# Attention outputs kept feature by token: no turns back, softmax sums and row scales applied as broadcast rows and columns

## The chip, the cores and the metric

One Trainium2 chip, and of it one core. The metric is the device time of one execution in microseconds. The kernel before takes 1211.41 us (median of three runs, 1211.18 to 1212.05).

## The reference

One transformer block over 1024 tokens and 1024 features. Half of the mixed width is attention (8 heads of 64), half is a gated recurrence (HGRN, 4 heads of 128).

```python
h = rmsnorm(x, mix_pre_norm[layer])
proj = h @ w_in[layer]
...
attn = dilated_mixture_attention(q_a.reshape(ahead), k_a.reshape(ahead), v_a.reshape(ahead), slopes)
attn = rmsnorm(attn.reshape(B, S, ATTN_WIDTH), attn_out_norm[layer])
rec = hgrn2_recurrence(q_h, f_h, i_h, g_h, lower_bounds[layer], hgrn_out_norm[layer])
mixed = jnp.concatenate([attn, rec], axis=-1) @ w_out[layer]
x = x + rmsnorm(mixed, mix_post_norm[layer])
h = rmsnorm(x, mlp_pre_norm[layer])
ff = jnp.square(jax.nn.relu(h @ w_ff1[layer])) @ w_ff2[layer]
x = x + rmsnorm(ff, mlp_post_norm[layer])
```

The attention mixes three patterns (dilations 1, 4 and 16), each a softmax over blocks, by their softmax sums. So for each token and head there is one sum of exponentials by which the output is divided, and for each token one row scale `ra` of the norm over all 512 attention features, with a gain for each feature.

## The kernel before

All large products are float32 in three passes: both operands are split into a rounded half (hi) and the rest (lo), and `three_pass` (L88 to L91) multiplies hi by hi, lo by hi and hi by lo. ACT rounds (L85) and DVE or POOL subtracts (L86).

The work has these stages: the projections and the recurrence; the eight attention heads in 64 steps (about 310 to 515 us); the output product, its norm and the residual by eight tiles of 128 tokens (515 to 591 us); and the two MLP products. PE runs one queue of instructions whose order the code writes by hand. A step s = 8 * head + i handles one of eight items (D0 to D3 for the first 512 tokens; F0, F1, N0, N1 for the others) of a head: scores for the coming item (`raise_`), their masked maximum on DVE (`look`), the exponential on ACT (L894), turns of the probabilities on PE (`turn`, L904 to L916), the products with the values (`weigh`), and in a later step `finish`. Between them `fill` puts pieces of a queue of other products into PE's order (keys and values of coming heads, and in the last heads `early_out`: the recurrent half of the output product of tiles 0 to 3, tiles `pwe`). The table `hooks` adds loads and passes at given steps. Steps 56 to 63 are head 7.

`weigh` gives the output of two heads' values as features by tokens, in PSUM. The value rows are split as well, so 128 partitions hold the hi part's and the lo part's product (64 each). ACT copies them into SBUF. `finish` (L978 to L996) turns 128 tokens at a time back by `TE.transpose` (L988: 2, 2 and 4 per head, 64 in all), DVE adds the two parts (L992), and POOL multiplies by the reciprocal `rd` of the softmax sums, which then are one number per token and so one per partition (L993). Pairs of heads collect in `anat` slabs and go to `mix_dram`, tokens by 1024 features; the last pair stays in SBUF.

The sums of the F items lie in another order of tokens than the rest. `send` (step 5) writes them to DRAM with their order changed, `receive` (step 6) reads them back (`swd`, `stat`, L856 and L859), and `finish` of the last item, in step 1 of the next head, adds them (L985) and takes the reciprocal. Two more tiles, `swap` (L867) and `px` (L875), carry row maxima to PE and back.

The output stage takes the attention features of a tile from `mix_dram` (`row_load`), sums their squares on ACT (`row_norm`), takes the scale on POOL, multiplies by the gain (POOL) and, for tiles 4 to 7, by the scale (`row_attn`, DVE), and turns the 512 features back by four transposes (`row_turn(t, 1)`, L1080, 32 in all), splitting them into hi and lo. `late_out` multiplies: 12 matmuls per half tile for tiles 0 to 3, whose recurrent half is there already, and 24 for tiles 4 to 7. `mixed_half` adds (tiles 0 to 3, with the scale) and squares for the norm behind it. `residual` and `next_turn` (tiles `ph`, `hraw`, `h2`) prepare the MLP for the tiles that are done.

DMAs go out from SP in one queue, in the order in which the code writes them, each behind the waits of the one ahead. Each of them uses one of eight semaphores in turn, so it also waits for the landing of the eighth before it. ACT, DVE and POOL work off one queue each, in order too.

## Time and profile before

| | |
|---|---|
| median of three runs | 1211.41 us |
| the profiled execution, its span | 1210.78 us, 1209.0 us |
| PE busy | 1198.8 us (99%) |
| DVE, ACT, POOL busy | 868.8, 546.6, 328.9 us |
| granted TensorE clock | 1.00 |
| heads, output loop | to 515.08 us; 515.08 to 591.21 us |

The span runs from the first to the last instruction. In lists of groups "x32" is a count and three numbers of a duration are shortest, median and longest, in ns. In timelines the first column is the start, the second the time busy, and brackets hold the idle time ahead and who ended it. Where a row carries several matmuls, its time runs from the first start to the last end. In the list of DMAs the last number is the time from issue to landing.

### The profile page before, as it was taken

Reading aid. Unit: us, or ns where it says so; the run is one execution under the profiler, and the core shown is the slowest. Engines: PE = TensorE matmul, PEld = TensorE weight load, DVE = VectorE, ACT = ScalarE, POOL = GpSimd, SP = SyncE. Lnnn points to the kernel's source line nnn. Section 1 sums busy time; section 2 is a strip of 40 time slices with the busy share of each in tenths; the row PEclk is TensorE's granted clock in tenths of the full one; section 3 lists DMA queues with packets and bytes.
Section 4 is the critical chain, followed back from the end, with each engine's and each line's share of the span. In section 5 each row is a group of like instructions: output and inputs, shape, how many; then the busy total and the mean of one; then the engine's idle time right before and its main releaser. Section 6 shows DMA issues by size and latency. Waiting matters only on the chain.

```text
span 1209.0 us, 17248 instructions
## 1 busy us (share of the span) xinstructions
PE 1198.8 (99%) x6350; PEld 1027.1 (85%) x6350; DVE 868.8 (72%) x1476; ACT 546.6 (45%) x1067; POOL 328.9 (27%) x323
## 2 busy tenths in 40 slices
PE   9999999999999999999999999999999999999998
PEld 8898989888888887888888888888888888888886
DVE  5697978777666767677689566766688554578796
ACT  7633333322665668855664222222234543534562
POOL 0110201022221215264330786575631000000022
PEclk9999999999999999999999999999999999999999
DMA  6231323123434445263514555553587534433337
GB/s 219 69 95 57 107 73 109 36 82 87 139 93 124 126 126 142 94 228 125 191 62 157 183 196 192 202 182 143 205 318 267 200 102 142 163 98 104 106 105 279
DMA packets 85716, 173.17 MB, mean 143 GB/s; under 512 B 12416, under 2 KB 38016, under 8 KB 85632
## 3 DMA queue, kind: packets, MB, share of 16 engines
q1 hardware_dynamic: 85632, 172.07, 42.9%
q8 instruction: 50, 0.82, 0.3%
q14 instruction: 34, 0.28, 0.1%
HBM read 117.76 MB, written 47.99 MB: 137 GB/s over the span
## 4 chain that ended last, share of the span: by engine, by line
PE 95%; ACT 2%; DVE 2%; issue 1%; POOL 0%; DVEq 0%; POOLq 0%; ACTq 0%
PE f L1947 18%; PE f2s L1947 7%; PE pig L91 2%; PE pig L89 2%; PE pig L90 2%; PE pl L480 2%; PE pwo L89 2%; PE pwo L91 2%; PE pwo L90 2%; PE pm_ak L89 1%; PE pm_f L89 1%; PE pm_ak L91 1%; PE pm_ak L90 1%; PE pm_f L91 1%; PE pm_f L90 1%; PE pm_av L89 1%
## 5 line engine op out<-in xcount | busy, mean ns | idle before, releaser
L86 DVE TENSOR_TENSOR al<-ar,ah 128x1024 fp32r<-128x1024 f32 x56 | 70.6, 1260 | 79.2 <-ACT ah L85 79.2
L1947 PE MATMUL f<-bh,ah 128*128 128x512 f32 x320 | 124.5, 389 | 0.0
L1947 PE MATMUL f<-bl,ah 128*128 128x512 f32 x320 | 124.5, 389 | 0.0
L1947 PE MATMUL f<-bh,al 128*128 128x512 f32 x320 | 124.5, 389 | 0.0
L85 ACT ACTIVATE ah<-ar 128x1024 fp32r<-128x1024 f32 x56 | 59.1, 1056 | 83.9 <-DMA ar<-actd 78.5
L1947 PEld LDWEIGHTS f<-bh,ah 128*128 128x128 f32 x320 | 60.1, 188 | 12.6
L1947 PEld LDWEIGHTS f<-bl,ah 128*128 128x128 f32 x320 | 60.1, 188 | 12.5
L1947 PEld LDWEIGHTS f<-bh,al 128*128 128x128 f32 x320 | 60.1, 188 | 12.3
L2021 POOL TENSOR_SCALAR lbl<-ssq 128x1 f32<-128x1 f32 x4 | 3.3, 820 | 245.7 <-ACT fd L2017 245.6
L1570 POOL TENSOR_TENSOR e<-x,e 128x512 f32<-128x512 f32 x14 | 21.6, 1540 | 131.0 <-DVE x L1521 131.0
L1947 PE MATMUL f2s<-bh,al 128*128 128x512 f32 (+1 forms) x128 | 48.9, 382 | 0.0
L1947 PE MATMUL f2s<-bl,ah 128*128 128x512 f32 (+1 forms) x128 | 48.9, 382 | 0.0
L1947 PE MATMUL f2s<-bh,ah 128*128 128x512 f32 (+1 forms) x128 | 48.9, 382 | 0.0
L673 POOL COPY tout<-traw 128x256 f32<-128x256 f32 x16 | 12.7, 792 | 106.6 <-DMA traw<-in_bias_tab_dram 76.2
L86 DVE TENSOR_TENSOR bl<-br,bh 128x1024 fp32r<-128x1024 f32 x32 | 40.1, 1252 | 1.4 <-ACT bh L85 1.3
L1964 ACT ACTIVATE acc<-f 128x512 f32<-128x512 f32 x28 | 16.7, 598 | 50.1 <-PE f L1947 50.1
L993 POOL TENSOR_TENSOR anat<-anat,stat 128x128 f32<-128x128 f32 (+1 forms) x24 | 12.4, 515 | 92.4 <-DVE anat L992 78.7
L85 ACT ACTIVATE bh<-br 128x1024 fp32r<-128x1024 f32 x32 | 33.6, 1051 | 5.0 <-PE f L1947 3.3
L86 DVE TENSOR_TENSOR wl<-raw,wh 128x1024 fp32r<-128x1024 f32 x21 | 27.2, 1295 | 8.9 <-ACT wh L85 8.9
L709 POOL TENSOR_TENSOR kl<-kf,kh 64x512 fp32r<-64x512 f32 x16 | 22.2, 1389 | 39.6 <-ACT kh L708 37.4
L753 POOL TENSOR_TENSOR ql<-qf,q 64x512 fp32r<-64x512 f32 x16 | 21.4, 1339 | 41.6 <-ACT q L752 41.0
L89 PE MATMUL pwo<-woh,mt 128*128 128x512 f32 x80 | 32.2, 402 | 0.0
(1703 smaller groups left out, 4030.0 us busy)
## 6 DMA issues: line engine op xcount, KB each, us to landing
ar<-actd SPq DMA_DIRECT2D x56, 512.0 KB, 3.5
br<-in_w_ff_dram SPq DMA_DIRECT2D x16, 1024.0 KB, 6.1
w1r<-in_w_ff_dram SPq DMA_DIRECT2D x14, 1024.0 KB, 6.4
raw<-in_w_in_dram SPq DMA_DIRECT2D x26, 512.0 KB, 3.6
actd<-e SPq DMA_DIRECT2D x17, 768.0 KB, 4.3
actd<-e SPq DMA_DIRECT2D x11, 1024.0 KB, 4.1
raw<-in_w_out_dram SPq DMA_DIRECT2D x8, 512.0 KB, 3.6
xres<-in_x_dram SPq DMA_DIRECT2D x8, 512.0 KB, 4.2
```

The costliest lines, as they stand in the source:

```text
L85: S.activation(hi, src, AF.Copy)
L86: eng.tensor_tensor(out=lo, in0=src, in1=f32(hi), op=ALU.subtract)
L89: TE.matmul(dst, lhs[0], rhs[0], start=start, stop=False)
L90: TE.matmul(dst, lhs[0], rhs[1], start=False, stop=False)
L91: TE.matmul(dst, lhs[1], rhs[0], start=False, stop=stop)
L480: TE.matmul(pl[:, n % 2, :192], kt[:, n * P:(n + 1) * P], sets[u // 2][:, n % 4], start=True, stop=True)
L673: G.tensor_copy(by_class(dst[:, part_ * w:(part_ + 1) * w]), in_blocks(raw[:, FAR * DIL:]))
L709: G.tensor_tensor(out=kl[a:b], in0=src, in1=f32(kh[a:b]), op=ALU.subtract)
L753: G.tensor_tensor(out=lo[a:b], in0=full[a:b], in1=f32(stacks[i]["q"][a:b, sl]), op=ALU.subtract)
L1570: eng[0].tensor_tensor(out=e1[:, 3], in0=a21, in1=e1[:, 2], op=ALU.add)
L1947: TE.matmul(pm, a[:, j, c], b[:, j, d], start=start and j == 0 and q == 0, stop=stop and j == 1 and q == 2, skip_group_check=True)
L1964: S.activation(acc_at(p, i), pm, AF.Copy)
```

## The change

`weigh` and `finish` no longer turn. ACT copies the 64 partitions of one part, and `finish` is one add on DVE, into a slab `o` of features by tokens for each pair of heads. The reciprocals go to DRAM as rows (`rd_dram`, 512 elements of 4 bytes a time) by `send_rows`, at step 3 for the first 512 tokens and at step 7 for the others, each from SP; the add that needs the received sums now stands there, at the end of step 7. The slabs of pairs 0 to 2 go to `o_dram`. `out_load` reads a pair back (`on`, 512 KB) with its reciprocals broadcast over 64 partitions per head (`rdr`, two of 256 KB). `out_scale` multiplies the two (POOL, 128x1024), `out_square` sums squares of the pairs into `osq` (POOL), `out_split` applies the gain as a column and splits (ACT and DVE), and its results go into the products as they are. `out_norm` gets the row scales by four 128x1 matmuls of `osq` with ones. Tiles 0 to 3 are scaled behind the product, as before. For tiles 4 to 7 the recurrent half is divided by the scale in PSUM (`late_rec`, ACT, both halves of a tile first), the attention half added on top, and the common factor goes into the `eps` of the norm behind.

```diff
     def weigh(hd, kind, g):
...
-            S.activation(ot, po[:, :256], AF.Copy)
+            S.activation(ot[a:b], po[c:d, :256], AF.Copy)
...
     def finish(hd, kind, g, po, ot):
...
-        if kind == "N":
-            V.tensor_tensor(out=st["xd"], in0=st["dn"][:, 4:8], in1=st["xd"], op=ALU.add)
-            V.reciprocal(st["rd"][:, 4:], st["xd"])
-        for u in range(n):
-            TE.transpose(po[:, o + u * P:o + (u + 1) * P], ot[:, u * P:(u + 1) * P], ident)
...
-        V.tensor_reduce(dst, pair.rearrange("p u a d -> p u d a"), axis=AX.X, op=ALU.add)
-        G.tensor_tensor(out=dst, in0=dst, in1=st["rd"][:, b].unsqueeze(2).to_broadcast([P, n, 64]), op=ALU.mult)
+        if kind == "D":
+            dst, src = outs[pr][a:b, g * 256:g * 256 + 256], po[a:b, :256]
+            V.tensor_tensor(out=dst, in0=src, in1=ot[a:b], op=ALU.add)
...
+        if hd % 2 and kind == "N" and pr < AH // 2 - 1:
+            nc.sync.dma_start(out=o_dram[pr], in_=outs[pr])
+
+    def send_rows(hd, hf):
+        st = stats[hd]
+        sl = slice(4 * hf, 4 * hf + 4)
+        if hf == 1:
             V.tensor_tensor(out=st["xd"], in0=st["dn"][:, 4:8], in1=st["xd"], op=ALU.add)
+            V.reciprocal(st["rd"][:, sl], st["xd"])
+        nc.sync.dma_start(out=rd_dram[hd][sl].rearrange("b p -> p b"), in_=st["rd"][:, sl])
...
+    def out_load(pr, hfs=(0, 1)):
+        if pr < AH // 2 - 1:
+            outs[pr] = slab("S", f"on{pr}")
+            nc.sync.dma_start(out=outs[pr], in_=o_dram[pr])
+        if 0 in hfs:
+            loaded[pr] = slab("S", f"rdr{pr}")
+        c = slice(512 * hfs[0], 512 * hfs[-1] + 512)
+        for i, (a, b) in enumerate(halves):
+            nc.sync.dma_start(out=loaded[pr][a:b, c], in_=rd_dram[2 * pr + i].rearrange("b p -> (b p)")[c].partition_broadcast(64))
+
+    def out_scale(pr, c=slice(0, T), eng=G):
+        eng.tensor_tensor(out=outs[pr][:, c], in0=outs[pr][:, c], in1=loaded[pr][:, c], op=ALU.mult)
+
+    def out_square(pr, c=slice(0, T), eng=G):
+        o = outs[pr][:, c]
+        if pr == 0:
+            scales["osq"] = slab("S", "osq")
+            eng.tensor_tensor(out=scales["osq"], in0=o, in1=o, op=ALU.mult)
             return
+        sq = loaded[pr][:, c]
+        eng.tensor_tensor(out=sq, in0=o, in1=o, op=ALU.mult)
+        eng.tensor_tensor(out=scales["osq"][:, c], in0=scales["osq"][:, c], in1=sq, op=ALU.add)
+
+    def out_split(pr, hf):
+        hi, lo = out_part(pr, hf)
+        src, gain = outs[pr][:, hf * 512:hf * 512 + 512], gains["cols"][:, pr:pr + 1]
+        S.activation(hi, src, AF.Copy, scale=gain)
+        V.scalar_tensor_tensor(lo, src, gain, f32(hi), op0=ALU.mult, op1=ALU.subtract)
+
+    def out_norm(hf):
+        pn = bank("t", f"pn{hf}")
+        for j in range(4):
+            t = 4 * hf + j
+            TE.matmul(pn[:, j:j + 1], scales["osq"][:, t * P:(t + 1) * P], f32(ones), start=True, stop=True)
...
+    def late_rec(t, hf):
...
+        for j in range(4):
+            three_pass(pm, [mts[t][:, i, j] for i in range(2)], [w[:, sl] for w in parts[WO0 + j]], j == 0, j == 3)
+        S.activation(pm, pm, AF.Copy, scale=scales["row", 1][:, t - NE:t - NE + 1])
...
-        55: lambda: [w_get(WO0 + 4, 0), row_load(0)],
-        57: lambda: [row_load(1), row_norm(0, (0,))],
...
+        51: lambda: out_load(0),
+        52: lambda: [row_turn(2), load_gain("gmix", "R", g_mix)],
+        53: lambda: [out_scale(0), out_square(0)],
+        54: lambda: [row_turn(3), out_split(0, 0), out_split(0, 1)],
+        55: lambda: out_load(1),
+        56: lambda: [out_scale(1), out_square(1)],
+        57: lambda: [out_split(1, 0), out_split(1, 1), out_load(2)],
+        58: lambda: out_scale(2),
+        59: lambda: [w_get(WO0 + 4, 0), out_square(2), out_split(2, 0)],
+        61: lambda: [w_get(WO0 + 5, 0), out_load(3, (0,))],
+        63: lambda: [w_get(WO0 + 6, 0), out_scale(3, FIRST), out_square(3, FIRST), out_split(3, 0)],
...
+        elif i == 7:
+            send_rows(hd, 1)
...
+    out_load(3, (1,))
     w_get(WO0 + 7, 0)
-    row_norm(2)
-    row_gain(2)
+    out_norm(0)
+    out_split(2, 1)
...
     for t in range(NT):
-        late_out(t, 0, last_rows if t == 0 else None)
+        if t >= NE:
+            late_rec(t, 0)
+            late_rec(t, 1)
+        late_out(t, 0)
+        if t == 0:
+            out_scale(3, SECOND, V)
+            out_square(3, SECOND)
+            out_split(3, 1)
+        elif t == 1:
+            out_norm(1)
```

The queue of SP around head 6's sums, first before (`etable` is a table of biases, `gmix` the gains as rows, `swd6` and `stat6` head 6's sums out and in, `raw` weights):

```order
L800 DMA etable_4793<-tabd7_643 128x704
L1004 DMA gmix_5290<-in_g_mix_dram 128x1024
L856 DMA swd6_650<-stat6_5012 128x4
L859 DMA stat6_5012<-swd6_650 128x4x1
L106 DMA raw34_5389<-in_w_out_dram 128x1024
L1030 DMA row0_5391<-mixd_135 128x384
```

and now (`rdd6` is head 6's reciprocals, sent in two parts; `on` and `rdr` as above):

```order
L803 DMA etable_4767<-tabd7_644 128x704
L1267 DMA cols_88<-in_g_mix_dram 128x4x1
L1003 DMA rdd6_662<-stat6_4974 128x4x1
L1058 DMA on0_5213<-od0_653 128x1024
L1063 DMA rdr0_5215<-rdd0_656 64x1024
L1063 DMA rdr0_5215<-rdd1_657 64x1024
L1011 DMA gmix_5254<-in_g_mix_dram 128x1024
L859 DMA swd6_651<-stat6_4974 128x4
L862 DMA stat6_4974<-swd6_651 128x4x1
L1003 DMA rdd6_662<-stat6_4974 128x4x1
L1058 DMA on1_5357<-od1_654 128x1024
L1063 DMA rdr1_5359<-rdd2_658 64x1024
```

Five DMAs have come in between `etable` and `gmix`, and the loads of pair 1 stand behind the second `rdd6`, which needs `stat6`.

The queue of ACT at step 57, in head 7, before (`pd7` to `pf7` are exponentials, `pth7` the rounded halves of turned probabilities, `dm0` a sum of squares over a loaded row):

```order
L933 ACTIVATE pth7_0_5412<-pt7_D1_5449 128x2x128
L1046 ACTIVATE dm0_5476,ass_5475<-row0_5391 128x384
L894 ACTIVATE pd7_5327,stat7_5326<-pd7_5327,stat7_5326 128x512
L933 ACTIVATE pth7_2_5496<-pt7_D2_5495 128x3x128
L953 ACTIVATE pf7_5328<-pov7_0_5506 128x256
L1046 ACTIVATE dm1_5513,ass_5512<-row1_5473 128x384
L894 ACTIVATE pf7_5328,stat7_5326<-pf7_5328,stat7_5326 128x192
L933 ACTIVATE pth7_2_5496<-pt7_D3_5521 128x4x128
```

and now:

```order
L936 ACTIVATE pth7_0_5381<-pt7_D1_5421 128x2x128
L1081 ACTIVATE othh_5043<-on1_5357,cols_88 128x512
L1081 ACTIVATE ot0_5327<-on1_5357,cols_88 128x512
L897 ACTIVATE pd7_5291,stat7_5290<-pd7_5291,stat7_5290 128x512
L936 ACTIVATE pth7_2_5465<-pt7_D2_5464 128x3x128
L958 ACTIVATE pf7_5292<-pov7_0_5475 64x256
L897 ACTIVATE pf7_5292,stat7_5290<-pf7_5292,stat7_5290 128x192
L936 ACTIVATE pth7_2_5465<-pt7_D3_5488 128x4x128
```

In the place of one pass over `row0` stand two over the scaled pair 1, ahead of the exponential `pd7` and the two `pth7` that PE's items use.

The queue of ACT in tile 6 of the output loop, before (`dx50` squares the residual of tile 5, `hraw` copies turned tiles out of PSUM, `dp60` squares the mixed tile 6, `h2h` rounds):

```order
L1161 ACTIVATE dx50_6350,x2h_6349<-xres5_6213 128x512
L1161 ACTIVATE dx51_6355,x2h_6349<-xres5_6213 128x512
L1192 ACTIVATE hraw00_6012<-ph23_0_6364 128x4x128
L1192 ACTIVATE hraw10_6021<-ph23_1_6370 128x4x128
L1132 ACTIVATE dp60_6377,pss_6376<-pwo6_0_6305 128x512
L1192 ACTIVATE hraw01_6409<-ph24_0_6404 128x4x128
L1192 ACTIVATE hraw11_6416<-ph24_1_6411 128x4x128
L1132 ACTIVATE dp61_6420,pss_6376<-pwo6_1_6379 128x512
L85 ACTIVATE h2h0_6013<-hraw00_6012 128x4x256
L85 ACTIVATE h2h1_6022<-hraw10_6021 128x4x256
```

and now:

```order
L1183 ACTIVATE dx50_6210,x2h_6209<-xres5_6087 128x512
L1183 ACTIVATE dx51_6215,x2h_6209<-xres5_6087 128x512
L1214 ACTIVATE hraw00_5900<-ph23_0_6224 128x4x128
L1214 ACTIVATE hraw10_5909<-ph23_1_6230 128x4x128
L1154 ACTIVATE dp60_6237,pss_6236<-pwo6_0_6157 128x512
L1214 ACTIVATE hraw01_6256<-ph24_0_6251 128x4x128
L1214 ACTIVATE hraw11_6263<-ph24_1_6258 128x4x128
L1154 ACTIVATE dp61_6267,pss_6236<-pwo6_1_6171 128x512
L1129 ACTIVATE pwo7_0_6275<-pwo7_0_6275,ora1_5748 128x512
L1129 ACTIVATE pwo7_1_6289<-pwo7_1_6289,ora1_5748 128x512
L86 ACTIVATE h2h0_5901<-hraw00_5900 128x4x256
L86 ACTIVATE h2h1_5910<-hraw10_5909 128x4x256
```

The two scalings of the recurrent halves of tile 7 (L1129) have come ahead of `h2h0`.

In PE's queue the four matmuls of `out_norm(0)` (L1088) now stand between the last `weigh` and the first product of tile 0, which followed it at once before.

189 lines of the change are left out of this document (78 added, 111 removed).

## The prediction

> **What bounds the kernel now.** I read the first part of the page (PE 99% busy, in the table above), then the busy time by stretch, then the list of PE's waits, then the timelines.
>
> ```profile
> 475.00:515.00 40.00, 39.26 (x256) 33.94 (x254) 27.41 (x85) 32.05 (x91) 11.33 (x19) 1.00 0.40 120
> 515.00:591.00 76.00, 76.00 (x385) 63.79 (x384) 56.01 (x73) 42.06 (x112) 35.68 (x69) 1.00 0.48 165
> ```
>
> The columns of the two stretches are the length and then the busy time of PE, PEld, DVE, ACT and POOL. PE is never idle in the output loop (515 to 591) and idle for 0.74 us in the last 40 us of the heads, where ACT is busy for 32 of 40. So a PE instruction taken away is time gained, and a PE wait put in is time lost. Between 300 and 606 us PE's waits are these and one of 0.2:
>
> ```profile
> PE pwe L89 <- DVE vf L766: 0.7, 1, 0.7
> PE pt_F L916 <- ACT pf L894: 0.6, 1, 0.6
> PE px L875 <- DVE swap L867: 0.3, 1, 0.3
> ```
>
> That is 1.8 us in total. There is almost no waiting to remove, and the margins behind it are thin: ACT and DVE deliver a few tenths of a microsecond ahead of PE.
>
> **What goes on PE.** Both kinds of turn are seen between three-pass matmuls.
>
> ```profile
> L988 PE MATMUL pov_far<-ident,pn x32: 271/273/273, 337.0 to 516.8; 128*128 128x128 f32 x32
> L988 PE MATMUL pov<-ident,pf x16: 270/272/273, 316.4 to 502.6; 128*128 128x128 f32 x16
> L988 PE MATMUL pov<-ident,pd x16: 272/283/299, 323.0 to 508.7; 128*128 128x128 f32 x16
> L1080 PE MATMUL pmt<-ident,row x48: 270/273/297, 511.2 to 572.2; 128*128 128x128 f32 x48
> ...
> 502.53 0.38 PE L988 MATMUL pov<-ident,pf 128*128 128x128 f32 x2
> 502.67 0.48 PE L89 MATMUL pwe<-wh,emt 128*128 128x512 f32 x1
> ...
> 516.51 0.60 PE L988 MATMUL pov_far<-ident,pn 128*128 128x128 f32 x4
> 516.94 0.60 PE L1080 MATMUL pmt<-ident,row 128*128 128x128 f32 x4
> 517.30 0.47 PE L89 MATMUL pwo<-woh,mt 128*128 128x512 f32 x1
> 517.61 0.39 PE L90 MATMUL pwo<-wol,mt 128*128 128x512 f32 x1
> 517.84 0.39 PE L91 MATMUL pwo<-woh,mt 128*128 128x512 f32 x1
> ```
>
> The durations (0.27 us) overlap; the starts give the price. Matmuls follow each other by 0.23 (517.61 to 517.84), but the one behind turns holds 0.31 (517.30 to 517.61). Two turns take 0.14 (502.53 to 502.67); with the 0.08, 0.22 a pair. Eight take 0.79 and the same 0.08: 0.87, so 0.44 for four. The 64 turns of `finish` go: 16 pairs, 3.5 us, and 8 fours, 3.5. The attention half of every output row is not turned: 32 of the 48 turns of L1080, 8 fours, 3.5 us. The eight 128x1 matmuls of `out_norm` come.
>
> ```profile
> 501.23 0.28 PE L875 MATMUL px<-pick,swap 128*128 128x4 f32 x2
> 501.37 0.63 PE L904 MATMUL pt_D<-ident,pd 128*128 128x128 f32 x4
> ```
>
> The nearest is this pair of 128x4, 0.14 us; so 0.6 us for eight, between nothing and the 0.9 of eight turns. Net 10.5 - 0.6 = **9.9 us less PE work**, of which 3.2 us lie in the output loop (8 fours less the second `out_norm`). The three-pass products keep their number and shape. POOL's small products (L993) and DVE's reductions (L992) go too, on engines with time to spare.
>
> **First new wait: DVE in heads 1 to 5.** `send_rows(hd, 1)` puts the add that needs the joined sums `xd` at the end of step 7; until now it stood two steps later.
>
> ```profile
> 366.40 0.16 DVE L985 TENSOR_TENSOR stat<-stat 128x4 f32<-128x4 f32 x1
> ...
> 357.95 0.38 SPq L859 DMA_DIRECT2D stat<-swd  x1
> ...
> 360.30 0.42 DVE L844 CUSTOM_DVE_ANT_0 pn<-ps_N,bt 128x256 f32<-128x256 f32 x1 [1.10 <-PE ps_N L840]
> ...
> DMA to landing us min/median/max: 1.4/3.4/5.8
> ```
>
> For head 1 the receive leaves at 357.95 and lands 3.4 later, at 361.4; the add is now ahead of the score pass of 360.30, which waits 1.1 us, and PE's next scores wait for its bank. Bounds: nothing, to 2.5 us a head. I take 2.8 for five heads. It hardly counts, because of what follows.
>
> **Second: the chain of head 6.** In the last head ACT's `out_split`, in its one queue, waits for POOL's `out_scale`, and that for two loads, which stand behind `send_rows(6, 1)` on SP.
>
> ```profile
> 480.03 0.43 SPq L995 DMA_DIRECT2D mixd<-anat  x1
> 480.51 0.58 SPq L800 DMA_DIRECT2D etable<-tabd  x1
> 482.78 0.56 SPq L856 DMA_DIRECT2D swd<-stat  x1
> ...
> gmix<-in_g_mix_dram SPq DMA_DIRECT2D x1, 512.0 KB, 7.3
> ...
> swd<-stat SPq DMA_DIRECT2D x1, 2.0 KB, 5.8
> stat<-swd SPq DMA_DIRECT2D x1, 2.0 KB, 2.3
> ...
> DMA to landing us min/median/max: 5.0/5.8/6.6
> L86 POOL TENSOR_TENSOR wl<-raw,wh 128x1024 fp32r<-128x1024 f32 x2 | 4.8, 2394 | 5.3 <-ACT wh L85 5.3
> ```
>
> Five more DMAs (`cols`, a send, `on0`, two `rdr0`) stand ahead of `swd6`, each 0.48 behind the last (480.03 to 480.51): it leaves at 485.2 and not 482.78. It lands 5.8 later, 491.0; the receive 2.3 later, 493.3; add and reciprocal 0.4; then the send, `on1` and two `rdr1`, the last issued at 495.1. A 256 KB broadcast (the smaller of the two `etable` rows) lands in 5.0: 500.1. Bounds are 2.3 (a small row that meets an idle queue) and `gmix`' 7.3. POOL multiplies 128x1024 in 2.4: 502.5. ACT splits a half in 0.6, DVE follows with 0.7 for each of two halves: 504.4 (estimates from the 128x512 passes of both engines). DVE then has score passes and the sums of head 7 to do before the `swap` of PE's second `px`:
>
> ```profile
> 499.24 0.36 DVE L844 CUSTOM_DVE_ANT_0 pf<-ps_F,etable 128x192 f32<-128x192 f32 x1 [0.26 <-PE ps_F L840]
> ...
> 500.19 0.38 DVE L867 TENSOR_TENSOR swap<-stat,pick 128x128 f32<-128x128 f32 x1
> ```
>
> That is 1.3 us: PE's `px` starts at 505.7, where it now starts at 501.23. Without the chain it would have come 6.5 us early less the first waits, near 498.5. **So all that PE saved until here is lost, and 4.5 us more**, whatever its exact amount. The first `out_scale` (step 54) waits in the same way, 2 us, and lies inside this.
>
> **Third: the norm ahead of the products.**
>
> ```profile
> 515.08 0.45 PE L89 MATMUL pwo<-woh,mt 128*128 128x512 f32 x1
> ...
> 511.63 0.33 SPq L106 DMA_DIRECT2D raw<-in_w_out_dram  x1
> ...
> L1037 POOL TENSOR_TENSOR erows<-erows,etable x4: 1285/1340/2311, 457.0 to 477.9; 128x512 f32<-128x512 f32 x4
> ```
>
> From `px` to the first product are 13.85 us now, 0.9 less without two pairs and a four; POOL is still busy with pair 1 (two squares of 2.4) when ACT asks for pair 2, 0.9 us more. The heads would end at 519.5. But `out_norm(0)` needs pair 3's first half scaled, squared and added by POOL, and its `rdr3` is loaded behind `raw35` on SP, 511.63 + 4.5 + 0.9 = 517.0, so issued by 517.8. I let it land in the 3.4 of the middle `swd` row, 521.2, and POOL takes three times 1.34: 525.2. PE waits 5.7 us. With the four small matmuls the products start at 525.5, **10.4 us later than now**. Bounds: 2 us of waiting, if the row lands at once and POOL keeps to 1.28; 9 if it lands in 5 and POOL takes 1.9.
>
> **The output loop.** It has 3.2 us less PE work, but `late_rec` puts both recurrent halves of tiles 4 to 7 first, and their PSUM scaling (L1129) into ACT's queue.
>
> ```profile
> 572.30 1.04 PE L1186 MATMUL ph<-ident,esum 128*128 128x128 f32 x8
> ...
> 578.64 1.04 PE L1186 MATMUL ph<-ident,xres 128*128 128x128 f32 x8
> ...
> 577.60 1.06 ACT L1192 ACTIVATE hraw<-ph 128x512 f32<-128x512 f32 x2
> ...
> 580.82 2.02 ACT L85 ACTIVATE h2h<-hraw 128x1024 fp32r<-128x1024 f32 x2
> ...
> 590.41 1.22 DVE L86 TENSOR_TENSOR wl<-raw,wh 128x1024 fp32r<-128x1024 f32 x1
> ```
>
> Between the turns of tile 3 (572.30) and of tile 4 (578.64), which share banks, stand 24 matmuls; now 12, 2.8 us less. ACT's first copy out of the bank ends at 578.13, 0.5 ahead of PE, and it waits for DVE's residual and not for PE: PE waits 2.2. Then `h2h`, 2.2 us behind 578.64, comes to stand behind the scaling of `pwo7_1`, that is 24 matmuls, some 7.2 us behind; the `wl` that it delays by 5.0 ends at 591.63, 2.9 ahead of its matmul (f11a, about 594.5): 2.1 more. Bounds: 0 to 5 together. The loop is then worth -3.2 + 4.3 = +1.1.
>
> **Costed at nothing.** The copy of half the partitions and one add in `finish` stand where a full copy and a reduction stood, on ACT and DVE. The store of `o_dram` takes the place of that into `mix_dram`, on the same queue. The other sends of rows (512 elements of 4 bytes) go out while SP has nothing to issue; if one met a landing like `swd`'s 5.8, only its reader `rdr` would wait, a head or more later. In tiles 0 to 3 the row scale stays where it was; in tiles 4 to 7 it is the ACT pass that the loop's sum holds. DVE loses the gain passes of the attention rows, which no wait of PE rests on.
>
> **Sum.** 10.4 + 1.1 = +11.5 on the profiled execution's 1210.78 (span 1209.0): 1222. That execution is 0.63 below the median of 1211.41, less than I can resolve.
>
> **The skill on two of these rows.** By the Trainium skill (GPSIMD Engine Reference, 8. Key points) GpSimd shares its SBUF interfaces with VectorE and contends with its instructions that read two SBUF inputs. L1037 agrees as far as it goes: median 1.34, once 2.31. By that rule POOL's adds beside DVE's splits would stretch by up to 1.7, and the sum would be some 1.7 us for pair 1 and 2.8 for pair 3 higher, 1227. By the skill's TensorE: Matmul & The Clock Gate (HAM oscillation), a PE gap over 3.4 us halves the clock until a window is busy again; two such gaps would give an estimated 3.4 us, 1225. The clock stays at 1.00 here, and no run has such a gap.
>
> **Rivals.**
> - **Covered.** Loads and POOL come in time, PE keeps its 9.9: 1201. It decides at 496: if `rdr1` has landed by then, px is not held. Against it: `swd` alone took 5.8 us there. 0.07.
> - **Half covered.** `swd6` lands in its shortest 1.4 and the broadcast sooner, so px goes at about 499; the norm still waits 5, the loop stays: px 499 + 13.0 of heads, but `rdr3` issued by 510.2, 3.4, 4.0 and 0.3: products at 517.9, 2.8 late, and +1.1: 1214.7. Without the loop's waits 1210, and 1207 with the norm's wait at its lower bound. 0.13.
> - **More.** POOL at 1.7 times its time, or the loads at `gmix`' 7.3, or a clock that drops behind the waits: 2.3 for the loads, up to 4.5 for POOL, 2 for `rdr3`: 1228 to 1233. 0.16 (POOL 0.07, loads 0.05, clock 0.04).
> - **Forecast**, 1214 to 1228: 0.64. That the turns save less PE time than worked out changes little here, for the saving before 501 is lost anyway.
>
> **Numbers.** 1222; the range 1207 to 1231 leaves out the covered case and the end of the last one. Within 0.2% (2.4 us, about what a measurement tells from no change): 0.08; faster 0.11 (the covered case and a third of the half covered), slower 0.81.
>
> **What would show it.** No L988; `px` waiting about 4.5 us for DVE's swap near 505, with ACT idle before L1081 for POOL; the 128x1 matmuls waiting about 5 us for POOL near 525; POOL 2.4 for 128x1024; `ph` waiting for `hraw` near 585. I am wrong if `rdr1` lands before 497, if POOL is done before the last `weigh`, or if the loop is shorter than now by more than 3 us.

## The result, and the profile after

The changed kernel takes **1296.45 us** (median of six runs, 1295.31 to 1297.33), beside 1211.37 for the kernel before in the same session (1211.18 to 1212.05): 1.070 times as long, 95% interval 1.0686 to 1.0714. That is 85 us slower. The forecast was 1222 with a range of 1207 to 1231: the direction was right and the size far off.

The first part and the slices of the page say where it is lost. (The slices are 32 us long, so the heads are slices 10 to 18.)

```profile
PE 1213.5 (94%) x6270; PEld 1034.8 (80%) x6270; DVE 874.0 (68%) x1471; ACT 548.2 (42%) x1043; POOL 333.0 (26%) x284
...
PE   9999999999999977448989999999999999999998
...
PEclk9999999999999988878999999999999999999999
...
DMA packets 92626, 175.28 MB, mean 135 GB/s; under 512 B 21504, under 2 KB 43520, under 8 KB 92544
```

PE is busy for 94% of the span instead of 99%. Of its 80.8 us of idle time, 50 lie between 475 and 606 us, in the last heads and the output loop, and 16 more in the heads ahead of them (310 to 475); there the granted clock, which was 1.00 everywhere before, falls as well. Here are the same two stretches of time as in the prediction, and the list of PE's waits (microseconds in total, times, longest):

```profile
475.00:515.00 40.00, 30.26 (x171) 25.06 (x170) 23.66 (x69) 24.63 (x68) 12.05 (x8) 0.89 0.64 123
515.00:591.00 76.00, 40.02 (x202) 34.30 (x201) 34.37 (x71) 27.43 (x63) 24.03 (x12) 0.74 0.60 75
```

```profile
PE px L878 <- DVE swap L870: 16.5, 1, 16.5
PE ps_N L842 <- DVE stat L847: 16.3, 6, 6.9
PE pn L1088 <- POOL osq L1076: 12.3, 2, 8.2
PE ps_D L842 <- DVE stat L847: 11.1, 1, 11.1
...
PE ph L1208 <- ACT hraw L1214: 2.0, 1, 2.0
...
PE f11a L1533 <- DVE wl L87: 1.4, 1, 1.4
...
PE pwo L90 <- DVE ad L1169: 1.2, 1, 1.2
```

The waits stand at the places that the prediction names: `px` of the last head, the banks of the N scores, the small matmuls of the norm, `ph` and `f11a`. But `px` waits 16.5 us and not 4.5, and the N scores 16.3 and not 2.8. The timelines show the chain behind `px`; the brackets hold the idle time ahead of each instruction and who ended it:

```profile
550.10 2.34 POOL L1066 TENSOR_TENSOR on<-on,rdr 128x1024 f32<-128x1024 f32 x1 [18.51 <-DMA rdr<-rdd]
...
552.48 0.72 ACT L1081 ACTIVATE othh<-on,cols 128x512 fp32r<-128x512 f32 x1 [13.04 <-POOL on L1066]
...
553.23 1.73 DVE L1082 SCALAR_TENSOR_TENSOR othl<-on,cols,othh 128x512 fp32r<-128x512 f32 x1 [11.81 <-ACT othh L1081]
554.88 2.82 DVE L1082 SCALAR_TENSOR_TENSOR ot<-on,cols,ot 128x512 fp32r<-128x512 f32 x1
...
560.28 0.59 PE L878 MATMUL px<-pick,swap 128*128 128x4 f32 x2 [16.52 <-DVE swap L870]
```

This is the predicted chain, link by link: load, POOL's scale, ACT's split, DVE's split, `swap`, `px`. What is furthest off is its first link, the load (DVE's two splits are longer than the 0.7 us each that were predicted as well; more of this below). Before looking at it, the span of 85.2 us is taken apart. PE's idle time grew from 10.1 to 80.8 us, which is +70.7. PE's busy time grew from 1198.8 to 1213.5. Of that busy time the trace has 43.6 us at a granted clock of 0.50; counted as half, the work at full clock is 1191.7 us, 7.1 less than before, and the lower clock costs 21.8. So: **+70.7 waiting, +21.8 lower clock, -7.1 work** (the rest to 85.2 is rounding).

Now SP's issues around the second send of head 5 (a timeline: start, time that the issue took), and then the row on landing for that send alone and for the four `vd` stores behind it:

```profile
495.30 0.38 SPq L1003 DMA_DIRECT2D rdd<-stat  x1
498.62 1.75 SPq L728 DMA_DIRECT2D vd<-v  x4
500.46 9.77 SPq L647 DMA_DIRECT2D vf<-vd  x6
```

```profile
L1003 SPq DMA_DIRECT2D rdd<-stat x1: 383/383/383, 495.3 to 495.3; - x1
...
DMA to landing us min/median/max: 10.3/10.3/10.3
L728 SPq DMA_DIRECT2D vd<-v x4: 330/423/433, 498.6 to 499.9; - x4
...
DMA to landing us min/median/max: 7.4/7.7/7.8
```

A send of 2 KB takes 10.3 us and lands at 505.6. Of the four stores behind it the trace has the landing of three: they take 7.4 to 7.8 us, where the same four take 1.7 to 2.5 in the trace of before, and land at 506.4 to 506.9, directly behind the send. SP issues the six `vf` loads in 9.8 us, where it needs 4.3 without the send (in the kernel with no sends, below). The row of all issues of a kind (count, KB each, median microseconds to landing of those whose landing the trace has) points the same way; for the sends it rests on three of 16, which took 8.6, 9.1 and 10.3:

```profile
rdd<-stat SPq DMA_DIRECT2D x16, 2.0 KB, 9.1
swd<-stat SPq DMA_DIRECT2D x8, 2.0 KB, 10.3
...
on<-od SPq DMA_DIRECT2D x3, 512.0 KB, 12.1
```

The 16 sends of 512 four-byte elements are new traffic of 32 KB altogether. **Theory W** is that they, and not the loads or the new arithmetic, cost most of the 85 us: what is issued behind one lands behind it. W2 says why they are slow: small writes side by side in DRAM. The rivals are that the loads of 256 KB are slow in themselves, that a load waits for its own sums, and that the new waits of DVE, ACT and POOL cost the time whatever the DMAs do.

### The profile page after: what moved, and what is told of

It is laid out like the page before. It is cut to its first block, busy times and chain, and to the rows that moved or that the text cites. A ratio compares the mean times of both kernels' runs of the same rounds, so it can differ in the third digit from the quotient of the medians.

```text
span 1294.2 us, 17042 instructions
## 1 busy us (share of the span) xinstructions
PE 1213.5 (94%) x6270; PEld 1034.8 (80%) x6270; DVE 874.0 (68%) x1471; ACT 548.2 (42%) x1043; POOL 333.0 (26%) x284
## 2 busy tenths in 40 slices
DMA packets 92626, 175.28 MB, mean 135 GB/s; under 512 B 21504, under 2 KB 43520, under 8 KB 92544
## 4 chain that ended last, share of the span: by engine, by line
PE 51%; DMA 4%; DVE 2%; ACT 1%; POOL 1%; issue 1%; SPq 0%; DVEq 0%; POOLq 0%; ACTq 0%
PE f L1976 17%; PE f2s L1976 7%; DMA rdr<-rdd 1%; PE pwo L90 1%; PE pwo L92 1%; PE pwo L91 1%; DMA gmix<-in_g_mix_dram 1%; DMA rdd<-stat 1%; DMA swd<-stat 1%; DVE ad L1169 0%; POOL on L1066 0%; DVE h2l L87 0%; DVE xres L1170 0%; PE ph L1208 0%; DVE othl L1082 0%
## 5 line engine op out<-in xcount | busy, mean ns | idle before, releaser
L712 POOL TENSOR_TENSOR kl<-kf,kh 64x512 fp32r<-64x512 f32 x16 | 22.2, 1389 | 99.0 <-ACT kh L711 83.5
L87 DVE TENSOR_TENSOR wl<-raw,wh 128x1024 fp32r<-128x1024 f32 x21 | 25.7, 1222 | 7.3 <-ACT wh L86 7.1
L87 DVE TENSOR_TENSOR bl<-tt,bh 128x1024 fp32r<-128x1024 f32 x24 | 29.3, 1220 | 1.5 <-ACT bh L86 1.5
L90 PE MATMUL pm_ak<-hTh,wh 128*128 128x512 f32 x64 | 28.2, 441 | 0.0
```

The costliest lines, as they stand in the source:

```text
L87: eng.tensor_tensor(out=lo, in0=src, in1=f32(hi), op=ALU.subtract)
L90: TE.matmul(dst, lhs[0], rhs[0], start=start, stop=False, **kw)
L712: G.tensor_tensor(out=kl[a:b], in0=src, in1=f32(kh[a:b]), op=ALU.subtract)
```

## Experiments

Each was run beside the kernel before, which took 1210.85 to 1211.19 us. Times are of one execution each; differences under 2.4 us are not read. "Idle" and "full" are PE's idle time and its work at full clock, worked out as above.

| kernel | us | PE idle | PE busy at clock 0.50 | full |
|---|---|---|---|---|
| before | 1211.37 | 10.1 | 0 | 1198.8 |
| changed | 1296.45 | 80.8 | 43.6 | 1191.7 |
| changed, sends unread | 1293.28 | 75.1 | 48.8 | 1191.9 |
| changed, no sends | 1238.56 | 36.3 | 15.0 | 1193.0 |
| sends 512 bytes apart | 1247.94 | 43.2 | 22.2 | 1191.8 |
| sends 64 bytes apart | 1245.69 | 43.8 | 14.8 | 1192.7 |
| sends as 16-byte runs | 1246.55 | 41.0 | 24.9 | 1191.3 |
| sends from POOL | 1277.27 | 62.7 | 39.5 | 1192.7 |
| before, with the sends | 1238.50 | 29.9 | 15.8 | 1198.9 |
| sends as 128-byte rows | 1250.56 | 45.4 | 22.5 | 1192.2 |

### Are the sends to blame, and for what?

**Sends as they are, read by nobody.** The loads of `rdr` take a row of gains in place of the sums, so the outputs are scaled by other numbers; everything is issued as in the change.

```diff
-            nc.sync.dma_start(out=loaded[pr][a:b, c], in_=rd_dram[2 * pr + i].rearrange("b p -> (b p)")[c].partition_broadcast(64))
+            nc.sync.dma_start(out=loaded[pr][a:b, c], in_=g_mix[c].partition_broadcast(64))
```

> Sends as in the change; the broadcast loads read a row of gains in place of the sums, so no load waits for a send (the attention scaling is wrong). Theory W: the queue is held all the same, 1275 to 1300. Rival R (it is the loads' waits for their sends that cost): about 1222 to 1240.

Measured: 1293.28 us, 3 less than the change. The sends take 9.5 us, and the loads of pairs behind them still 11 (again medians of the few whose landing is known, three sends and two loads):

```profile
on<-od SPq DMA_DIRECT2D x3, 512.0 KB, 11.0
...
rdd<-stat SPq DMA_DIRECT2D x16, 2.0 KB, 9.5
```

So the wait of a load for the sums that it reads is worth 3 us at most.

**No sends at all.** The same edit, and `send_rows` keeps its add and reciprocal and sends nothing:

```diff
-        nc.sync.dma_start(out=rd_dram[hd][sl].rearrange("b p -> p b"), in_=st["rd"][:, sl])
```

> As a3, without the 16 sends. Theory W: 1210 to 1225, landings as in the kernel before. Rival B (slow broadcast loads): 1260 or above, with rdr landing in 10 us or more. Rival D (the earlier add on DVE): some 1270.

Measured: 1238.56 us, 54.7 less than with unread sends. PE's waits are now of the size that the prediction spoke of (`ph`, `f11a` and `pwo` as in the change):

```profile
PE pn L1087 <- POOL osq L1075: 6.5, 1, 6.5
PE ps_D L842 <- DVE stat L847: 6.0, 1, 6.0
PE ps_N L842 <- DVE stat L847: 3.6, 4, 1.5
PE px L878 <- DVE swap L870: 2.5, 1, 2.5
```

and SP issues the loads of the far values without a stop:

```profile
475.70 4.28 SPq L647 DMA_DIRECT2D vf<-vd  x6
```

**The sends alone, on the kernel before.** These are the change's sends and nothing else of it, and nobody reads them; the second send of a head stands at step 1 of the next head, where this kernel has its reciprocals, and not at step 7.

```diff
             V.reciprocal(st["rd"][:, 4:], st["xd"])
+            nc.sync.dma_start(out=rd_dram[hd][4:].rearrange("b p -> p b"), in_=st["rd"][:, 4:])
...
             joint(hd, 1)
+            nc.sync.dma_start(out=rd_dram[hd][:4].rearrange("b p -> p b"), in_=stats[hd]["rd"][:, :4])
```

> The kernel before, all as it was, with nothing of the change but its row sends: 16 DMAs of 512 four-byte elements side by side, at step 3 for the first half and in finish of the last item (step 1 of the next head) for the second; nobody reads them, the output is the reference's. Theory W (a send of small writes holds what is issued behind it, whoever reads it): each send lands 8 to 14 us after its issue, swd's median goes from 3.4 to over 5, row and weight loads behind a send land 8 us and more later, and since PE has almost no wait to lose, the kernel is slower: 1220 to 1260, with the clock below 1.00 behind the longest waits. Rival (the sends hurt only through the new chain of loads, scale and split, which is not there): 1209 to 1214, and PE's waits as before.

Measured: 1238.50 us, 27.7 more than the kernel before, for 32 KB of stores. Its sends take 10.6 us (the median of six with a known landing), its `swd` up to 17.5 (here the row gives shortest, median and longest of `swd` and its receive), and PE waits where it never did:

```profile
PE pt_N L914 <- DVE ptNl L935: 6.8, 1, 6.8
PE pt_N L914 <- ACT pn L895: 5.3, 2, 4.7
PE pt_F L917 <- ACT pf L895: 4.8, 3, 3.5
```

```profile
DMA to landing us min/median/max: 2.1/6.3/17.5
```

With that the four corners are there: neither 1211, the sends alone +27.7, the rest of the change alone +27.5, both +85.1. The parts add up to 55; **30 us come only from the two together**. A likely reason is that the new chain (load, scale, split, `swap`, `px`) begins with the very loads that the sends hold; that was not tested by itself, and the other place of the second send is in this figure too. This kernel also tests the accounting of the clock: it runs the same PE instructions as before, PE is busy for 1206.8 us, and the work at full clock comes out at 1198.9, beside 1198.8.

### What makes a send slow?

Three kernels send the same 512 numbers of four bytes in other ways. The first two leave the loads on gains, as above; in the third the sums reach the loads in a scrambled order.

```diff
-    rd_dram = [dp.tile([NT, P], F32, name=f"rdd{hd}") for hd in range(AH)]
+    rd_dram = [dp.tile([NT, P, P], F32, name=f"rdd{hd}") for hd in range(AH)]
...
-        nc.sync.dma_start(out=rd_dram[hd][sl].rearrange("b p -> p b"), in_=st["rd"][:, sl])
+        nc.sync.dma_start(out=rd_dram[hd][sl, :, 0].rearrange("b p -> p b"), in_=st["rd"][:, sl])
```

**512 bytes apart:**

> Four-byte sends as before, but each element 512 bytes from the next in DRAM; the loads read a row of gains in place of the sums (the attention scaling is wrong). Theory W1 (the price is one of each small write by itself): the sends land in 9 us or more, 1280 to 1300. Theory W2 (many small writes into one line are put one behind the other): they land in 2 to 5 us, about 1222.

**64 bytes apart** (the tile is `[NT, P, 16]`):

> As the kernel with 4-byte sends 512 bytes apart (1247.9; sends landed in 2.1 us), but the elements lie 64 bytes apart; the loads read gains in place of the sums, as there. If 64 bytes between two small writes are enough, the sends land in about 2 us and the time is 1244 to 1252. If small writes are slow whenever they fall in the same 512 bytes (eight of them do here, where 128 did in the change), the sends land in 4 us or more and the time is 1258 to 1293.

**As 128 runs of 16 bytes, one per partition, side by side in the same 2 KB:**

```diff
+        nc.sync.dma_start(out=rd_dram[hd][sl].rearrange("b p -> (b p)").rearrange("(p b) -> p b", p=P), in_=st["rd"][:, sl])
```

> The sends write the same 512 numbers to the same 2 KB, but as 128 runs of 16 bytes (in token order within a partition, so the softmax sums that come back are in a wrong order). Theory W (a send of 512 four-byte elements takes 9 to 14 us to land and holds everything behind it on SP's queue): the sends land in 2 to 4 us, swd in 3 to 6, and the time falls to about 1222 (1214 to 1232), which is what was predicted with ordinary landings. Rival B (the broadcast loads of 4 KB over 64 partitions are the slow transfers): stays at 1285 or above. Rival D (the add of the received sums two steps earlier on DVE is what costs, whatever the sends do): some 1270.

Measured: 1247.94, 1245.69 and 1246.55 us. The landings (shortest, median, longest) of the sends 512 bytes apart:

```profile
DMA to landing us min/median/max: 1.8/2.1/5.5
```

64 bytes apart:

```profile
DMA to landing us min/median/max: 1.8/2.2/4.1
```

as 16-byte runs, where the row of the issues gives the median alone (1.9):

```profile
rdd<-stat SPq DMA_DIRECT2D x16, 2.0 KB, 1.9
```

The spaced sends write just as many elements as the slow ones (both have the change's 21504 packets under 512 bytes) and land in 2.1 and 2.2 us and not in 9 to 10. So W2 holds: neither the number of small writes nor their size makes the price by itself, but that four-byte writes stand side by side, 16 of them in the same 64 bytes; with four longer ones there (the 16-byte runs) it is small. Spacings under 64 bytes were not tried, so the size of the stretch that they must not share is not known, and what in the memory or in the DMA engines makes it slow stays open. Against the kernel with unread sends the spacing alone is worth 45 us or more.

Fast sends are not free either: these three kernels are 7 to 9 us slower than the one with no sends, and PE waits 8.9 to 11.8 us in `px` there and 2.5 without sends. Where that comes from was not separated.

The Trainium skill (DMA: Bandwidth & Descriptors, Rules for kernel authors) says that a strided last dimension becomes one descriptor per element and should be rearranged. The trace agrees on the count, 9088 packets more under 512 bytes, and 8448 more than in the kernel with no sends (21504 and 13056), which is 528 for each send of 512 elements; but the runs set the price elsewhere, since with the same count and 64 bytes of room it falls to a quarter. The Trainium skill (DMA: Bandwidth & Descriptors, Specifications) states a read-modify-write for transfers under 512 bytes; small writes that stand 64 bytes apart land in 2.2 us here, so by themselves they do not show it.

### Does another queue help?

The prediction thought of SP's queue. If only the order of that queue held the loads, sends issued by another engine would let them pass.

```diff
-        nc.sync.dma_start(out=rd_dram[hd][sl].rearrange("b p -> p b"), in_=st["rd"][:, sl])
+        nc.gpsimd.dma_start(out=rd_dram[hd][sl].rearrange("b p -> p b"), in_=st["rd"][:, sl])
```

> The change as it is, but the row sends (4-byte elements, side by side) are issued from GpSimd and not from SP, all else the same. Theory W in its first form (what is held is the queue: loads land late because they stand behind a slow write in SP's queue): the sends still take 9 to 14 us themselves, but swd, vd and rdr land as without sends (swd median about 3.4, rdr 4 to 8), and only the two loads of a pair whose own send has just gone out wait for it; px waits 5 to 10 us: 1243 to 1260. Rival E (the slow write occupies the DMA engines or the memory, whatever its queue): swd median near 5.8 and rdr at 10 and over as in the change, 1280 to 1300.

Measured: 1277.27 us, above what W in its first form gave and a little below the rival. A send takes about as long as before: 8.8 us in the median of 12 with a known landing. (The trace counts 32 packets for such a send and not 528, 13568 under 512 bytes in all, so the number of packets does not make the price either.) Here is one of them, issued by POOL at 396.8, with two small stores that SP issues at 398.9 and 402.4:

```profile
L1003 POOL DMA_DIRECT2D rdd<-stat x1: 752/752/752, 396.8 to 396.8; - x1
...
DMA to landing us min/median/max: 8.3/8.3/8.3
L715 SPq DMA_DIRECT2D kl<-kl x2: 591/604/616, 398.9 to 402.4; - x2
...
DMA to landing us min/median/max: 3.2/4.7/6.3
```

The send lands at 405.0; the two stores at 405.2 and 405.6, although they stand in another queue; stores of `kl` take 2.4 us in the kernel with no sends. It is so with all 15 DMAs of SP in this trace that are issued while a send is under way and whose landing is known: each lands behind the send, 8.7 us after its issue in the median. So **the first form of W fell: it is not the queue that is held, but what the queues share**; whether that is the DMA engines or the memory behind them, the runs do not tell. Where the 19 us are gained was not separated: PE's waits for `px` and `ps_D` are 2.5 and 4.2 us here, where they were 16.5 and 11.1, and a new one of 9.9 stands at the far values. That sends from another queue hold SP's DMAs too agrees with the Trainium skill (DMA: Bandwidth & Descriptors, Issuing engines are not separate DMA queues), by which DMAs of all issuers run on the same 16 engines.

### Mending the sends

**128-byte rows.** DVE turns the sums in blocks of 32 by 32, and four DMAs of four rows of 128 bytes each take the place of one send.

```diff
-        nc.sync.dma_start(out=rd_dram[hd][sl].rearrange("b p -> p b"), in_=st["rd"][:, sl])
+        turned = half(f"rt{hd}{hf}")[:, :32]
+        V.transpose(out=turned, in_=st["rd"][:, sl].unsqueeze(1).to_broadcast([P, 8, 4]))
+        for i in range(4):
+            nc.sync.dma_start(out=rd_dram[hd][sl, 32 * i:32 * i + 32], in_=turned[32 * i:32 * i + 4])
```

> The sends are turned on DVE first and go out as four DMAs of four rows of 128 bytes each, so that no two writes share a line; the output is the reference's, and the reads are those of the change. Theory W2 (small writes beside each other are what is slow): the row sends land in 1.5 to 4 us, nothing behind them on SP is held, and the time is that of the kernel with the sums in scrambled order (1246.6), less a little because rows of 128 bytes are one packet each: 1238 to 1250. If instead the number of DMAs or of packets counts (twelve more issues on SP a pair of heads at about 0.5 us), SP's queue is late in the last heads: 1255 to 1275, with px and pn waiting as in the change.

Measured: 1250.56 us, 46 less than the change and half a microsecond above what was expected for rows that do not meet. Against the 16-byte runs (1246.55) the 12 more issues for each pair of heads and DVE's turn cost 4.0 us. The trace of this kernel has no landings, so those of the rows could not be read.

**Work put into a wait.** On top of it, 24 matmuls that nobody reads, ahead of the norm:

```diff
+    spare = bank("s", "idle")
+    for _ in range(8):
+        three_pass(spare, [mts[3][:, i, 0] for i in range(2)], [w[:, :512] for w in parts[WO0]], True, True)
     out_norm(0)
```

> As the kernel before it on this list, with 24 matmuls of 128x128 by 128x512 whose result nobody reads, put ahead of the four small matmuls of the norm; that is 5.5 us of PE work at full clock (24 by 0.23) in a place where PE waits 5.8 to 6.5 us for POOL. Theory C (an idle PE halves its own clock, and that costs on top of the wait): the wait shrinks to about 1 us, the clock stays near 1.00 between 530 and 550 us where it stood at 0.56 to 0.87, and the kernel is 2 to 6 us faster than the one without the extra matmuls, although it does 5.5 us more PE work. Rival (the lower clock has another cause, or the wait only moves behind the extra work): the same time or up to 5.5 us slower, with the clock as low as before.

Measured: 1246.88 us, 3.7 less with more work. The window from 540 to 550, in which PE comes back from the norm (PE, PEld, DVE, ACT and POOL busy, then the clock), without the extra matmuls:

```profile
540.00:550.00 10.00, 4.03 (x17) 3.59 (x18) 7.78 (x9) 3.51 (x6) 5.03 (x4) 0.68 0.36 104
```

and with them:

```profile
540.00:550.00 10.00, 9.48 (x46) 7.68 (x45) 7.41 (x10) 4.17 (x6) 5.45 (x5) 1.00 0.56 167
```

The wait at the norm falls from 6.0 to 0.5 us, and at that place the clock stays at 1.00. Theory C holds there: the clock drops because PE is idle. The extra work is 5.5 us in a wait of 6.0. The 3.7 us are not so clearly its gain, for other waits (`px`, the N scores) came out 2.4 us shorter, and PE's loss to the clock over the whole kernel fell only from 11.2 to 10.4 us, for it now shows at 609 and 630 us as well, where it did not before.

**Two moves.** The add of the received sums and the second send stand again at step 1 of the next head, and the norm behind the second half of the first tile:

```diff
-        elif i == 7:
+        elif i == 7 and hd == AH - 1:
             send_rows(hd, 1)
+        if i == 1 and hd > 0:
+            send_rows(hd - 1, 1)
...
-    out_norm(0)
...
         late_out(t, 1)
+        if t == 0:
+            out_norm(0)
+            mixed_half(t, 0)
```

> The sends as rows of 128 bytes, and two steps moved: the add of the received sums and the second send go back to step 1 of the next head (for the last head they stay), and the four small matmuls of the first norm stand behind the second half of the first tile's output product, with the scaling of its first half behind them. The moves should remove the 4 waits for the banks of N scores (3.8 us), the wait at the norm (5.8) and the half clock behind it (3 to 5); px stays held by the first loads (5 to 9 us). Expected 10 to 15 us less than the kernel with the mended sends alone: 1226 to 1238. If the waits only move (PE waits for the norm behind the second half, or for a bank), the gain is under 5 us: 1236 to 1248.

Measured: 1244.8 us, only 5.8 less. The waits for the N scores and at the norm are gone and `px` fell from 9.3 to 3.2, but PE's wait for `ps_D` grew from 6.6 to 8.9 and new ones of 3 to 5 us stand at `pt_F`, `pt_N` and the first output products. Most of the waiting has moved.

**Later splits.** On top of that:

```diff
-        53: lambda: [out_scale(0), out_square(0)],
-        54: lambda: [row_turn(3), out_split(0, 0), out_split(0, 1)],
+        53: lambda: out_scale(0),
+        54: lambda: [row_turn(3), out_square(0)],
         55: lambda: out_load(1),
-        56: lambda: [out_scale(1), out_square(1)],
-        57: lambda: [out_split(1, 0), out_split(1, 1), out_load(2)],
-        58: lambda: out_scale(2),
-        59: lambda: [w_get(WO0 + 4, 0), out_square(2), out_split(2, 0)],
-        61: lambda: [w_get(WO0 + 5, 0), out_load(3, (0,))],
+        56: lambda: out_scale(1),
+        57: lambda: [out_split(0, 0), out_load(2)],
+        58: lambda: [out_split(0, 1), out_square(1)],
+        59: lambda: [w_get(WO0 + 4, 0), out_scale(2)],
+        60: lambda: [out_split(1, 0), out_square(2)],
+        61: lambda: [w_get(WO0 + 5, 0), out_split(1, 1), out_load(3, (0,))],
+        62: lambda: out_split(2, 0),
```

> As the kernel with row sends as 128-byte rows, the late add and the later norm (1244.8), with the splits of pairs 0 to 2 asked for three to four steps later (0 at steps 57 and 58, 1 at 60 and 61, 2 at 62), and the squares behind the next step's scale. Theory Q (what is left is ACT's one queue: a split that waits for POOL and for a load of 5 to 8 us holds the exponentials behind it, DVE waits for ACT, and PE for DVE): ACT's wait for POOL in the heads falls from 13.6 to under 4 us, PE's waits for ps_D (8.9), px (3.2), pt_F and pt_N (8) to under 8 in sum, and with the clock that no longer drops the time is 1218 to 1232. Rival T (the loads, which come one pair after the other at 6 to 8 us each, end too late whatever the queue): the waits move to the first output products, and the time stays at 1238 to 1250.

Measured: 1236.64 us, 8.2 less, short of what theory Q gave and a little better than its rival's lowest. ACT's wait for POOL in the heads, in the kernel without this edit:

```profile
ACT othh L1084 <- POOL on L1069: 13.6, 3, 9.0
```

and with it:

```profile
ACT woh L86 <- POOL osq L1079: 7.8, 1, 7.8
...
ACT othh L1084 <- POOL on L1069: 1.1, 1, 1.1
```

ACT no longer waits in `othh`, and PE's waits for `ps_D` are gone and for `px` down to 0.9. But now the rounding of a weight slab waits 7.8 us for POOL, and PE waits 5.3 us for `wol` and 5.6 for `ptFl`. Theory Q is right on the waits that it names and wrong on the time: ACT's queue is not all that is left.

**The output loop.** On top of that, the recurrent product of a tile's second half stands between its two attention halves:

```diff
         if t >= NE:
             late_rec(t, 0)
-            late_rec(t, 1)
         late_out(t, 0)
...
+        if t >= NE:
+            late_rec(t, 1)
         late_out(t, 1)
```

> As the kernel with the later splits, and in the output loop the recurrent product of a tile's second half goes between its two attention halves and not ahead of both. The waits at the turns of the residual (ph, 2.0 us) and at the first product behind the loop (f11a, 1.4) should go, as the prediction's fifth term explains them by 12 matmuls in place of 24 between two turns: 2 to 4 us less than that kernel. If these waits have another cause: the same within 1 us.

Measured: 1252.29 us, 15.7 **more**. The waits for `ph` and for `f11a` are gone, as expected, but a larger one takes their place:

```profile
PE pwo L90 <- ACT pwo L1132: 18.6, 8, 6.1
```

ACT divides the recurrent half in PSUM before the attention half may be added on top. With both recurrent halves first, 12 matmuls cover that pass; with one right ahead of its attention half, nothing does, and PE waits at all eight halves. (As PE comes later to everything behind such a wait, the kernel does not show by itself that the order had caused the waits for `ph` and `f11a`.) The order in the change bought something that the prediction had not counted.

None of these kernels comes near the kernel before; the best of those that leave nothing out, 1236.64, is 25.5 us behind its neighbour run of the kernel before (1211.19).

## Why the prediction was wrong

**The step that failed** is the one under "Costed at nothing": "The other sends of rows (512 elements of 4 bytes) go out while SP has nothing to issue; if one met a landing like `swd`'s 5.8, only its reader `rdr` would wait, a head or more later." Both halves are wrong. SP does pause behind the send of 495.30, for 2.9 us, but the send is under way for 10.3. And not only its reader waits: every DMA that is issued while a send is under way and whose landing is known lands behind it (9 of 9 in the change, 15 of 15 with the sends from POOL), the stores and loads of far values and of keys among them. That is 54.7 us here (the change with unread sends against none). The row of `swd`, of the same 2 KB, was no guide: `send` writes four neighbouring elements per partition, that is 128 runs of 16 bytes, and this is the form that lands in 1.9 us above. Same bytes, same queue, same neighbours, but a quarter of the writes.

Point by point:

- **PE work, -9.9.** Measured -7.1, and -4.9 to -7.5 in the other kernels with the change's PE work (a half clock is counted as half, which is coarse). Of the difference some 1.0 is the norm: it takes 16 matmuls and not 8, and eight of them 0.81 us at full clock (547.10 to 547.91 in the rows further below), so 1.6 for all and not 0.6. The rest was not separated.
- **DVE in heads 1 to 5, 2.8.** Without sends 3.6 us in 4 waits; right in kind and nearly in size. With them 16.3.
- **The chain of head 6, 4.5.** The links are as told. Without sends `px` waits 2.5; but the first `out_scale`, put at 2 us and hidden, makes `ps_D` wait 6.0, since the loads of pair 0 land 7.7 to 8.1 us after their issue and not 5: a weight slab, a store, a table, the two loads and the gains, 2.9 MB, are issued within 6 us. With the N scores that is 12.1 us of waiting ahead of `px`'s products, where the prediction implied 11 (4.5, and the 6.5 of saved work that were to be lost): near, but by luck, for the terms lie in other places.
- **DVE's splits in that chain, 0.7 each.** In the changed kernel they take 1.73 and 2.82 us (the timeline above), while POOL squares and adds: 3.1 us more on the way to `px`. In the traces the same pass takes 0.73 to 0.75 us where POOL does nothing beside it, and up to 2.95 where it does; POOL's multiply of 128x1024 takes 2.34 to 2.78 in the change, as predicted. So the contention of POOL and DVE that the prediction weighed is there, but here DVE pays for it.
- **The norm, 5.7.** Without slow sends 5.8 to 6.6. Right. (In the changed kernel it is 8.2, and the second norm waits 4.1 more.)
- **The output loop, 2.2 and 2.1.** 2.0 and 1.4. Right, with one wait of 1.2 (`pwo` for `ad`) not seen. That the cause is the order of `late_rec` fits the kernel that moves it, but is not shown by it, for in that kernel PE is late from other waits.
- **The clock.** A rival with a chance of 0.04. It came true: 21.8 us in the changed kernel.
- **Small slips in the sums.** The three prices of the rival "More" add up to 8.8 and so to 1231, not 1233; the `px` without the chain comes to 497.5 (501.23 - 6.5 + 2.8), not 498.5. Neither changes the forecast.

For the kernel without sends the sum can be checked: 27.8 us on the span, of which +26.2 waiting, -5.8 work and +7.5 clock (half of 15.0), with rounding. The prediction's own +11.5 was 21.4 of waiting less 9.9. So even without the sends it would have been 16 us short: 4.8 of waiting, 4.1 of work and 7.5 of clock.

How the clock behaves is seen in a window of the changed kernel, in which PE is idle for most of the time, and in matmuls of the kernel without sends behind its wait at the norm and at the second norm:

```profile
547.60:564.40 16.80, 4.12 (x13) 3.54 (x14) 9.11 (x15) 5.63 (x13) 13.92 (x6) 0.50 0.29 74
```

```profile
534.79 1.87 PE L1087 MATMUL pn<-ones,osq 128*128 128x1 f32 x8 [6.49 <-POOL osq L1075]
...
537.09 0.63 PE L91 MATMUL pwo<-wol,othh 128*128 128x512 f32 x1
537.52 0.63 PE L92 MATMUL pwo<-woh,othl 128*128 128x512 f32 x1
...
547.10 0.95 PE L1087 MATMUL pn<-ones,osq 128*128 128x1 f32 x8
547.91 0.49 PE L90 MATMUL pwo<-woh,othh 128*128 128x512 f32 x1
```

Behind the wait the matmul of 128x512 takes 0.63 us and follows the one ahead by 0.43 (537.09 to 537.52), where it took 0.39 and 0.23 at full clock (the rows in the prediction). In the trace of the change the stretches at 0.50 are 3.4, 6.8, 10.2 and 17.1 us long, multiples of 3.4, and in the kernel without sends the half clock goes on for 6.6 us behind the end of the wait, to 541.4. The prediction cited a rule for this from the Trainium skill (TensorE: Matmul & The Clock Gate, HAM oscillation), by which a gap over 3.4 us halves the clock, and thought it worth 3.4 us. The trace agrees with the rule for long waits: six of the eleven stretches in the span of the change behind the start-up begin inside waits of 4.1 to 16.5 us. It does not agree for the other five, which follow waits of 1.4 to 2.7 us. What decides for the short waits stays open: the wait of 2.0 at `ph` is followed by a half clock in the change and by none in the kernel without sends. So two sizes were wrong: the number of stretches, two against eleven, and their length, for the three of the kernel without sends last 6.8, 3.4 and 10.2 us.

The chances failed in the same place: every rival was built on the chain that was foreseen, and none on the traffic that was costed at nothing, though the diff showed 16 new DMAs of a shape that had no row in the trace.

## What to carry to other kernels

A DMA that is new in shape has no price in the old trace: bound it by itself, and ask what is issued while it is under way, not only who reads it. A column of four-byte numbers that goes from the partitions to DRAM side by side is such a shape; turn it first, or leave 64 bytes between the elements, if the reader can take them so. A kernel whose PE never waits can pay for a new wait twice, once for the wait (70.7 us here) and once for the half clock around it (21.8).

## What the runs showed of the hardware

- 512 writes of four bytes, side by side over 2 KB of DRAM: 8.8 to 10.6 us in the medians of four kernels (three to 12 sends with a known landing in each). With 64 or 512 bytes between them: 2.2 and 2.1. As 128 runs of 16 bytes, side by side: 1.9.
- While such a send is under way, DMAs issued by another engine in another queue land behind it too (15 of 15), the closest of them 0.2 us after it.
- Reading is another matter: `receive` reads 512 four-byte elements in an order as scattered, and lands in 2.3 us (the row in the prediction; 3.1 in the median of all eight in that kernel).
- DVE's split of 128x512 takes 0.73 to 0.75 us alone and up to 2.95 beside a POOL pass over 128x1024.
- 32 KB of such sends, read by nobody, made a kernel of 1211 us 27.7 us slower.
- All 42 waits of PE of 3.3 us or more in these 13 kernels, behind the start-up, brought half clock, in stretches of 3.4 us; of the 45 waits of 1.5 to 2.9 us, 18 did not. Matmuls put into the wait at the norm kept the clock at 1.00 there.
